# A 2x2x2 mean pool: all loads first on one DMA queue in 32 KB rows, all stores behind them

## The chip, the cores and the metric

The kernel runs on one core of a Trainium2 chip. Times are device microseconds (us) of one execution; lower is better. The kernel before takes 97.47 us, the median of three runs (97.29 to 97.55). A profile is one execution recorded by the hardware profiler; its span runs from the first to the last instruction of the program, and it is shorter than the measured time, because some time lies outside of it.

## What is computed

The input holds 8 x 32 volumes of 32 x 32 x 32 float32 numbers (33.55 MB). Each output number is the mean of a 2 x 2 x 2 block (4.19 MB in all).

```python
batch, channels, d, h, w = (8, 32, 32, 32, 32)
...
window = x[:, :, d_s:d_s + 2, h_s:h_s + 2, w_s:w_s + 2]
result[:, :, i, j, k] = np.mean(window, axis=(-3, -2, -1))
```

## The kernel before

The 256 volumes are taken in two halves of 128, one volume to a partition of the on-chip memory. A volume is a contiguous run of 128 KB in device memory. A half is cut along its depth into chunks of four planes (16 KB per partition, 2 MB over all partitions); the last chunk of the second half is cut again into two of two planes (8 KB per partition, 1 MB). There are 15 large and 2 small chunks.

`process_chunk` handles one chunk. Line 44 loads it, on the queue of SyncE (SP). VectorE (DVE) then makes three passes: line 50 adds planes in pairs (4096 numbers per partition become 2048), line 55 adds neighbours in a row (1024 are left), and line 59 adds rows in pairs, multiplies by 0.125 and writes 512 numbers into `obuf`, the output of the half; its unused sum goes to `dummy`, with a short instruction that reads the sum out. No other engine computes.

Outputs leave on the queue of ScalarE (ACT). When 14 of the 16 output planes of a half are done, line 91 stores them in one transfer (14 KB per partition, 1.84 MB). For the first half line 94 stores the other two planes in one transfer of 256 KB; for the second half lines 96 and 94 store one plane each (128 KB).

Three things set the order. SP issues loads in program order, and load n waits until the buffer that it reuses has been read by line 50: the pool `pin` has six buffers of 16 KB per partition, so up to six loads (12 MB) are queued. The stores stand on another queue, and run beside whatever loads are under way when they are issued. Each transfer also uses one of eight completion semaphores in turn (`DMAHW0` to `DMAHW7` below), and waits until its earlier user is done. Both queues feed the same 16 DMA engines.

Of the kernel before, what the change touches and what calls it, by code (L numbers as in the profile page):

```python
# [1 line left out]

# [4 lines left out]


@with_exitstack
def kernel(  # L10
    ctx: ExitStack,
    tc: tile.TileContext,
    x: bass.AP,
    kernel_size: int,
    out: bass.AP,
):
    nc = tc.nc
    assert kernel_size == 2, "only kernel_size == 2 supported"

    B, C, D, H, W = x.shape  # L20
    Do, Ho, Wo = D // 2, H // 2, W // 2
    N = B * C
    P = nc.NUM_PARTITIONS
    assert N % P == 0
    T = N // P

    xv = x.rearrange("b c d h w -> (b c) d h w")
    ov = out.rearrange("b c d h w -> (b c) d h w")

    HW = H * W  # L30

    add = mybir.AluOpType.add

    pool_in = ctx.enter_context(tc.tile_pool(name="pin", bufs=6))
    pool_mid = ctx.enter_context(tc.tile_pool(name="pmid", bufs=3))
    pool_out = ctx.enter_context(tc.tile_pool(name="pout", bufs=2))

    MAXDD = 4

    def process_chunk(xt, obuf, d0, DD, do0):  # L40
        OD = DD // 2
        tin_full = pool_in.tile([P, MAXDD * HW], mybir.dt.float32, tag="tin")
        tin = tin_full[:, : DD * HW]
        nc.sync.dma_start(out=tin, in_=xt[:, d0:d0 + DD, :, :])  # L44

        tin_v = tin.rearrange("p (od dd h w) -> p od dd h w", od=OD, dd=2, h=H, w=W)

        t1 = pool_mid.tile([P, (MAXDD // 2) * HW], mybir.dt.float32, tag="t1")
        t1 = t1[:, : OD * HW].rearrange("p (od h w) -> p od h w", od=OD, h=H, w=W)
        nc.vector.tensor_add(out=t1, in0=tin_v[:, :, 0], in1=tin_v[:, :, 1])  # L50

        t1_v = t1.rearrange("p od h (k ww) -> p od h k ww", ww=2)
        t2 = pool_mid.tile([P, (MAXDD // 2) * H * Wo], mybir.dt.float32, tag="t2")
        t2 = t2[:, : OD * H * Wo].rearrange("p (od h k) -> p od h k", od=OD, h=H, k=Wo)
        nc.vector.tensor_add(out=t2, in0=t1_v[:, :, :, :, 0], in1=t1_v[:, :, :, :, 1])  # L55

        t2_v = t2.rearrange("p od (j hh) k -> p od j hh k", hh=2)
        dummy = pool_mid.tile([P, 1], mybir.dt.float32, tag="dummy")
        nc.vector.tensor_tensor_reduce(  # L59
            out=obuf[:, do0:do0 + OD, :, :],  # L60
            in0=t2_v[:, :, :, 0, :],
            in1=t2_v[:, :, :, 1, :],
            scale=0.125,
            scalar=0.0,
            op0=add,
            op1=add,
            accum_out=dummy,
        )

    for t in range(T):  # L70
        xt = xv[t * P:(t + 1) * P]
        ot = ov[t * P:(t + 1) * P]

        obuf = pool_out.tile([P, Do, Ho, Wo], mybir.dt.float32, tag="obuf")

        if t == T - 1:
            chunks = [4] * (D // 4 - 1) + [2, 2]
            bulk_at = len(chunks) - 3
        else:
            chunks = [4] * (D // 4)  # L80
            bulk_at = len(chunks) - 2
        n = len(chunks)

        d0 = 0
        for ci, DD in enumerate(chunks):
            do0 = d0 // 2
            process_chunk(xt, obuf, d0, DD, do0)

            hi = do0 + DD // 2
            if ci == bulk_at:  # L90
                nc.scalar.dma_start(out=ot[:, 0:hi, :, :], in_=obuf[:, 0:hi, :, :])
            elif ci > bulk_at:
                if ci == n - 1:
                    nc.scalar.dma_start(out=ot[:, do0:, :, :], in_=obuf[:, do0:, :, :])
                else:
                    nc.scalar.dma_start(out=ot[:, do0:hi, :, :], in_=obuf[:, do0:hi, :, :])
            d0 += DD


# [1 line left out]
_INS = ['x', 'kernel_size']  # L101
_OUTS = [((8, 32, 16, 16, 16), 'float32')]
#: Inputs that are plain numbers.
_NUMBERS = {'kernel_size': 2}


# [26 lines left out]
```

## Time and profile before

| what | value |
|---|---|
| median of three runs | 97.47 us (97.29 to 97.55) |
| span of the profiled execution | 95.5 us |
| VectorE busy | 67.6 us (71% of the span), 68 instructions |
| data read and written | 33.55 MB and 4.19 MB, 395 GB/s over the span |
| queue of the loads (q1) | 2448 packets, 83.9% of 16 engines' span |
| queue of the stores (q10) | 720 packets, 10.6% of 16 engines' span |

The profile states no time of its own for the profiled execution beside the span. The span is 1.9 us below the median of the runs without a profiler, and this 1.9 us is taken as what lies around it. The three lines of digits in the page cut the span into 40 slices of 2.4 us: a digit is the busy share of a slice in tenths, and the row GB/s is what the DMA engines moved. A transfer's time "to landing" runs from its issue to the completion that the waiting engine sees. There is only one core, and its granted TensorE clock is 1.000 throughout; TensorE is not used.

### The profile page before, as it was taken

Reading aid. Unit: us, or ns where it says so; the run is one execution under the profiler, and the core shown is the slowest. Engines: PE = TensorE matmul, PEld = TensorE weight load, DVE = VectorE, ACT = ScalarE, POOL = GpSimd, SP = SyncE. Lnnn points to the kernel's source line nnn. Section 1 sums busy time; section 2 is a strip of 40 time slices with the busy share of each in tenths; the row PEclk is TensorE's granted clock in tenths of the full one; section 3 lists DMA queues with packets and bytes.
Section 4 is the critical chain, followed back from the end, with each engine's and each line's share of the span. In section 5 each row is a group of like instructions: output and inputs, shape, how many; then the busy total and the mean of one; then the engine's idle time right before and its main releaser. Section 6 shows DMA issues by size and latency. Waiting matters only on the chain.

```text
span 95.5 us, 151 instructions
## 1 busy us (share of the span) xinstructions
DVE 67.6 (71%) x68; POOL 0.2 (0%) x4
## 2 busy tenths in 40 slices
DVE  0006979797979797979439409879795979799920
POOL 0000000000000000000000000000000000000000
DMA  4899999999999999999999999999999999991993
GB/s 103 343 432 439 439 439 439 439 432 439 439 405 412 418 425 432 439 439 329 362 412 439 428 418 440 424 439 432 432 429 425 439 425 429 398 422 55 384 384 110
DMA packets 3169, 37.76 MB, mean 395 GB/s; under 512 B 352, under 2 KB 608, under 8 KB 736
## 3 DMA queue, kind: packets, MB, share of 16 engines
q1 hardware_dynamic: 2448, 33.56, 83.9%
q10 hardware_dynamic: 720, 4.19, 10.6%
q14 instruction: 1, 0.01, 0.0%
HBM read 33.55 MB, written 4.19 MB: 395 GB/s over the span
## 4 chain that ended last, share of the span: by engine, by line
DMA 79%; DVE 16%; issue 0%; SPq 0%; DVEq 0%
DMA tin_full<-in_x_dram 64%; DMA out_dram<-obuf 15%; DVE t L50 10%; DVE t L55 4%; DVE obuf L59 2%; DVE dummy L59 0%; SPq L44 0%; DVEq L128 0%
## 5 line engine op out<-in xcount | busy, mean ns | idle before, releaser
L50 DVE TENSOR_TENSOR t<-tin_full 128x2048 f32<-128x2048 f32 (+1 forms) x17 | 36.8, 2165 | 22.8 <-DMA tin_full<-in_x_dram 22.8
L55 DVE TENSOR_TENSOR t<-t 128x1024 f32<-128x1024 f32 (+1 forms) x17 | 19.7, 1162 | 0.5
L59 DVE CUSTOM_DVE_ANT_1 obuf<-t 128x512 f32<-128x512 f32 (+1 forms) x17 | 11.2, 660 | 0.5
L59 DVE DVE_READ_ACCUMULATOR2_ANT dummy<- 128x1 f32 x17 | 1.4, 82 | 0.0
L114 POOL MEMSET const-bfloat16-1.0<- 128x1 bf16 x1 | 0.1, 101 | 0.0
L114 POOL MEMSET const-uint8-127<- 128x1 uint8 x1 | 0.1, 101 | 0.0
L114 POOL MEMSET const-float32-0.0<- 128x1 f32 x1 | 0.1, 98 | 0.2 <-issue 0.2
L114 POOL MEMSET const-float32-1.0<- 128x1 f32 x1 | 0.1, 98 | 0.0
## 6 DMA issues: line engine op xcount, KB each, us to landing
tin_full<-in_x_dram SPq DMA_DIRECT2D x15, 2048.0 KB, 27.0
out_dram<-obuf ACTq DMA_DIRECT2D x2, 1792.0 KB, 10.1
tin_full<-in_x_dram SPq DMA_DIRECT2D x2, 1024.0 KB, 24.1
out_dram<-obuf ACTq DMA_DIRECT2D x1, 256.0 KB, 15.0
out_dram<-obuf ACTq DMA_DIRECT2D x2, 128.0 KB, 4.1
```

What stands on the lines that cost most here:

```text
L50: nc.vector.tensor_add(out=t1, in0=tin_v[:, :, 0], in1=tin_v[:, :, 1])
L55: nc.vector.tensor_add(out=t2, in0=t1_v[:, :, :, :, 0], in1=t1_v[:, :, :, :, 1])
L59: nc.vector.tensor_tensor_reduce(out=obuf[:, do0:do0 + OD, :, :], in0=t2_v[:, :, :, 0, :], in1=t2_v[:, :, :, 1, :], scale=0.125, scalar=0. ...
L114: nc = _bacc.Bacc("TRN2", target_bir_lowering=False, num_devices=1)
```

## The change

Loads now go to buffers of 32 KB per partition, eight planes (4 MB) each; the pool has five of them, 20 MB. A table `plan` lists eight such buffers: the first is filled by two transfers of 16 KB per partition, the next six by one transfer of 32 KB each, and the last by transfers of 16, 8 and 8 KB. DVE works on the same pieces as before, four planes at a time and two planes at the end (`pool_unit`), so that two units are cut out of one 32 KB transfer. The intermediates `t1` and `t2` have one buffer in place of three. The outputs of both halves stay in two buffers of 16 KB per partition, and all stores stand behind the last load in the program, on the same queue as the loads: the whole first half (2.10 MB), then 14 planes of the second half (1.84 MB), then its two last planes (131 KB each).

```diff
-    pool_in = ctx.enter_context(tc.tile_pool(name="pin", bufs=6))
-    pool_mid = ctx.enter_context(tc.tile_pool(name="pmid", bufs=3))
-    pool_out = ctx.enter_context(tc.tile_pool(name="pout", bufs=2))
...
+    pool_in = ctx.enter_context(tc.tile_pool(name="pin", bufs=5))
+    pool_mid = ctx.enter_context(tc.tile_pool(name="pmid", bufs=1))
+    pool_out = ctx.enter_context(tc.tile_pool(name="pout", bufs=1))
+    obuf = [pool_out.tile([P, 16 * KF], F32, name=f"obuf{t}") for t in range(2)]
+    plan = [
+        (0, 0, (16, 16)),
+        (0, 32, (32,)),
...
+        (1, 64, (32,)),
+        (1, 96, (16, 8, 8)),
+    ]
+    def load(t, k0, parts):
+        tin = pool_in.tile([P, 32 * KF], F32, tag="tin", name="tin")
+        o = 0
+        for kb in parts:
+            nc.sync.dma_start(
+                out=tin[:, o * KF:(o + kb) * KF],
+                in_=xv[t * P:(t + 1) * P, (k0 + o) * KF:(k0 + o + kb) * KF],
+            )
+            o += kb
+        return tin
...
+    for i, (t, k0, parts) in enumerate(plan):
+        tin = load(t, k0, parts)
+        o = 0
+        for kb in parts:
+            for u in range(0, kb, 16):
+                pool_unit(tin, t, k0, o + u, min(16, kb))
+            o += kb
...
-            if ci == bulk_at:
-                nc.scalar.dma_start(out=ot[:, 0:hi, :, :], in_=obuf[:, 0:hi, :, :])
...
+    for t, k0, kb in [(0, 0, 16), (1, 0, 14), (1, 14, 1), (1, 15, 1)]:
+        nc.sync.dma_start(
+            out=ov[t * P:(t + 1) * P, k0 * KF:(k0 + kb) * KF],
+            in_=obuf[t][:, k0 * KF:(k0 + kb) * KF],
+        )
```

`KF` is 256 numbers, 1 KB. `pool_unit` makes the three passes of `process_chunk` at lines 69, 74 and 78.

The first place is the tail of SP's program, from the load that reuses the third buffer to the end; the load lines are L44 before and L56 now, the stores are L95, and the semaphores and the DVE that a transfer waits for stand in brackets.

```order
-L44 DMA tin_full<-in_x_dram 128x4096 [waits DMAHW1_49,DMAHW0_49,DVE_49]
-L44 DMA tin_full<-in_x_dram 128x2048 [waits DMAHW3_49,DVE_49]
-L44 DMA tin_full<-in_x_dram 128x2048 [waits DMAHW4_49,DMAHW2_49,DVE_49]
-L128 UNCONDITIONAL_BRANCH
...
+L56 DMA tin<-in_x_dram 128x4096 [waits DMAHW3_49,DVE_49]
+L56 DMA tin<-in_x_dram 128x2048 x2
+L95 DMA out_dram<-obuf_64 128x4096 [waits DVE_49]
+L95 DMA out_dram<-obuf_65 128x3584 [waits DMAHW4_49,DVE_49]
+L95 DMA out_dram<-obuf_65 128x256 [waits DMAHW5_49,DVE_49]
+L95 DMA out_dram<-obuf_65 128x256 [waits DMAHW6_49,DVE_49]
+L129 UNCONDITIONAL_BRANCH
```

SP ended with its loads; now four stores stand behind them, each waiting for the DVE.

The second place is ACT's program, which held the five stores.

```order
-L91 DMA out_dram<-obuf 128x3584 [waits DMAHW0_49,DVE_49]
-L94 DMA out_dram<-obuf 128x512 [waits DMAHW2_49,DVE_49]
-L91 DMA out_dram<-obuf 128x3584 [waits DMAHW3_49,DVE_49]
-L96 DMA out_dram<-obuf 128x256 [waits DMAHW4_49,DVE_49]
-L94 DMA out_dram<-obuf 128x256 [waits DMAHW5_49,DVE_49]
```

None of them is left on that queue. The third place is DVE's end, where the last 16 KB piece of `tin` and the first 8 KB piece are worked on (t_169 and t_175 are intermediates).

```order
+L69 TENSOR_TENSOR t_169<-tin 128x2048 [waits DMAHW0_49]
+L74 TENSOR_TENSOR t_171<-t_169 128x1024 [waits DVE_49]
+L78 ISA obuf_65,dummy<-t_171 128x512 [waits DVE_49]
+L78 ISA dummy 128x1
+L69 TENSOR_TENSOR t_175<-tin 128x1024 [waits DMAHW1_49]
+L74 TENSOR_TENSOR t_177<-t_175 128x512 [waits DVE_49]
+L78 ISA obuf_65,dummy<-t_177 128x256 [waits DVE_49]
```

The same instructions stood there before, save that the pair addition of the 8 KB piece came one place earlier, ahead of the row addition of the 16 KB piece; now a unit ends before the next begins.

More of the change, by code (lines that the diff above doesn't have):

```diff
@@ L6 @@
 from concourse._compat import with_exitstack
+F32 = mybir.dt.float32
+KF = 256
 @with_exitstack
@@ L20 @@
     B, C, D, H, W = x.shape
-    Do, Ho, Wo = D // 2, H // 2, W // 2
-    N = B * C
     P = nc.NUM_PARTITIONS
[L24 to L30, printed above, removed]
-    add = mybir.AluOpType.add
-    pool_in = ctx.enter_context(tc.tile_pool(name="pin", bufs=6))
-    pool_mid = ctx.enter_context(tc.tile_pool(name="pmid", bufs=3))
-    pool_out = ctx.enter_context(tc.tile_pool(name="pout", bufs=2))
@@ L38 @@
[L38 to L67, printed above, removed]
-        )
@@ L70 @@
[L70 to L89, printed above, removed]
-            if ci == bulk_at:
[L91 to L97, printed above, removed]
+    assert (B * C, D, H, W) == (2 * P, 32, 32, 32)
@@ new lines @@
+    add = mybir.AluOpType.add
+    xv = x.rearrange("b c d h w -> (b c) (d h w)")
+    ov = out.rearrange("b c d h w -> (b c) (d h w)")
+    pool_in = ctx.enter_context(tc.tile_pool(name="pin", bufs=5))
[5 more added lines that the diff above has]
+        (0, 32, (32,)),
+        (0, 64, (32,)),
+        (0, 96, (32,)),
+        (1, 0, (32,)),
+        (1, 32, (32,)),
+        (1, 64, (32,)),
+        (1, 96, (16, 8, 8)),
+    ]
@@ new lines, in load, with pool_unit @@
+    def load(t, k0, parts):
[8 more added lines that the diff above has]
+        return tin
+    def pool_unit(tin, t, k0, o, kb):
+        od = kb // 8
+        a = tin[:, o * KF:(o + kb) * KF].rearrange("p (o dd e) -> p o dd e", o=od, dd=2)
+        t1 = pool_mid.tile([P, 8 * KF], F32, tag="t1", name="t1")
+        b = t1[:, :od * 1024]
+        nc.vector.tensor_add(
+            out=b.rearrange("p (o e) -> p o e", o=od), in0=a[:, :, 0], in1=a[:, :, 1])
+        bv = b.rearrange("p (e ww) -> p e ww", ww=2)
+        t2 = pool_mid.tile([P, 4 * KF], F32, tag="t2", name="t2")
+        c = t2[:, :od * 512]
+        nc.vector.tensor_add(out=c, in0=bv[:, :, 0], in1=bv[:, :, 1])
+        cv = c.rearrange("p (j hh k) -> p j hh k", hh=2, k=16)
+        dummy = pool_mid.tile([P, 1], F32, tag="dummy", name="dummy")
+        o0 = (k0 + o) * KF // 8
+        nc.vector.tensor_tensor_reduce(
+            out=obuf[t][:, o0:o0 + od * 256].rearrange("p (j k) -> p j k", k=16),
+            in0=cv[:, :, 0], in1=cv[:, :, 1],
+            scale=0.125, scalar=0.0, op0=add, op1=add, accum_out=dummy,
+        )
@@ L101 @@
+    tins = []
+    for i, (t, k0, parts) in enumerate(plan):
[10 more added lines that the diff above has]
+        )
 _INS = ['x', 'kernel_size']
```

## The prediction

> **What bounds the kernel now.** I read the page first: busy shares, slices, queues.
>
> ```profile
> span 95.5 us, 151 instructions
> DVE 67.6 (71%) x68; POOL 0.2 (0%) x4
> DMA  4899999999999999999999999999999999991993
> GB/s 103 343 432 439 439 439 439 439 432 439 439 405 412 418 425 432 439 439 329 362 412 439 428 418 440 424 439 432 432 429 425 439 425 429 398 422 55 384 384 110
> q1 hardware_dynamic: 2448, 33.56, 83.9%
> q10 hardware_dynamic: 720, 4.19, 10.6%
> ```
>
> The DMA engines are busy in nearly every slice, at a rate that rarely leaves 420 to 440 GB/s. DVE is idle for 29% of the span. So the bytes set the time, and what can be won is time in which the engines move less than they can: the ramp at the start, the dip in slices 18 to 20 (329, 362, 412), the hole in slice 36 (55) and the end. To size these I cut the span into stretches (columns: us, DVE busy and count, POOL, clock, DMA share, GB/s).
>
> ```profile
> 0.00:1.70 1.70, 0.00 (x0) 0.20 (x4) 1.00 0.00 0
> 4.00:42.10 38.10, 29.51 (x28) 0.00 (x0) 1.00 1.01 430
> 42.14:67.58 25.44, 16.86 (x16) 0.00 (x0) 1.00 1.00 412
> 67.58:82.74 15.16, 12.65 (x12) 0.00 (x0) 1.00 1.00 425
> 86.50:88.90 2.40, 2.37 (x5) 0.00 (x0) 1.00 0.02 7
> 88.90:94.20 5.30, 2.48 (x6) 0.00 (x0) 1.00 0.97 396
> 94.20:95.50 1.30, 0.00 (x0) 0.00 (x0) 1.00 0.00 0
> ```
>
> The last loads are through at 86.5, the last stores run from 88.9, and between them 2.40 us pass at 7 GB/s. The timeline tells why (start, duration, engine, line).
>
> ```profile
> 0.73 64.65 SPq L44 DMA_DIRECT2D tin_full<-in_x_dram  x17
> 7.89 2.29 DVE L50 TENSOR_TENSOR t<-tin_full 128x2048 f32<-128x2048 f32 x1 [7.89 <-DMA tin_full<-in_x_dram]
> 12.76 2.29 DVE L50 TENSOR_TENSOR t<-tin_full 128x2048 f32<-128x2048 f32 x1 [0.58 <-DMA tin_full<-in_x_dram]
> 37.24 2.29 DVE L50 TENSOR_TENSOR t<-tin_full 128x2048 f32<-128x2048 f32 x1 [0.61 <-DMA tin_full<-in_x_dram]
> 39.56 1.23 DVE L55 TENSOR_TENSOR t<-t 128x1024 f32<-128x1024 f32 x1
> 40.82 0.69 DVE L59 CUSTOM_DVE_ANT_1 obuf<-t 128x512 f32<-128x512 f32 x1
> 41.44 0.08 DVE L59 DVE_READ_ACCUMULATOR2_ANT dummy<- 128x1 f32 x1
> 41.55 0.38 ACTq L91 DMA_DIRECT2D out_dram<-obuf  x1
> 42.14 2.29 DVE L50 TENSOR_TENSOR t<-tin_full 128x2048 f32<-128x2048 f32 x1 [0.62 <-DMA tin_full<-in_x_dram]
> ...
> 67.58 2.29 DVE L50 TENSOR_TENSOR t<-tin_full 128x2048 f32<-128x2048 f32 x1 [0.57 <-DMA tin_full<-in_x_dram]
> 82.74 2.29 DVE L50 TENSOR_TENSOR t<-tin_full 128x2048 f32<-128x2048 f32 x1 [0.62 <-DMA tin_full<-in_x_dram]
> 88.07 0.34 ACTq L91 DMA_DIRECT2D out_dram<-obuf  x1
> 89.03 1.22 DVE L50 TENSOR_TENSOR t<-tin_full 128x1024 f32<-128x1024 f32 x1
> 91.36 0.08 DVE L59 DVE_READ_ACCUMULATOR2_ANT dummy<- 128x1 f32 x1
> 91.47 0.34 ACTq L94 DMA_DIRECT2D out_dram<-obuf  x1
> ```
>
> The second half's bulk store (L91 at 88.07) must wait for DVE, which got its chunk at 82.74 and is behind the loads at the end. The first half's store went out long before, at 41.55, into a stream of loads that already filled the engines: it gained nothing there, and nothing was left to fill the hole.
>
> **The rhythm.** From 12.76 to 42.14 DVE starts on six loads, always upon a landing: 29.38 / 6 = 4.897 us per 2 MB load (2.097 MB, so 428 GB/s). This is the price of a full stream. The lead ahead of it is 7.87 - 4.90 = 2.97 us. In 42.14 to 67.58 four loads land and the first half's 2.10 MB of stores leave, worth five such units, 24.49 us; it took 25.44, so 0.95 us is lost. In 67.58 to 82.74 three loads land, worth 14.69; 15.16 passed, 0.47 lost with no store about.
>
> **Stores: from issue to landing.**
>
> ```profile
> L91 ACTq DMA_DIRECT2D out_dram<-obuf x2: 339/359/379, 41.6 to 88.1; - x2
> DMA to landing us min/median/max: 5.9/10.1/14.4
> L94 ACTq DMA_DIRECT2D out_dram<-obuf x2: 338/338/338, 46.5 to 91.5; - x2
> DMA to landing us min/median/max: 3.1/9.1/15.0
> ```
>
> The bulk store of the end lands 5.9 us after issue; 1.835 MB at the stream's 428 GB/s is 4.29, so 1.6 lies around it. The very last lands at 91.47 + 3.1 = 94.57, and the span ends 0.93 later.
>
> **The change, part by part.** The bytes are the same. I follow the stream, and call T the landing of the last load.
>
> Loads: 16 units of 4.897 with nothing between them put T at 2.97 + 78.35 = 81.3. The supply holds: the five buffers are 20 MB, more than the 12 MB now queued, and DVE frees a buffer of 4 MB in 8.4 us (a unit is 41.44 - 37.24 = 4.20 us, and the next may start beside the read of the sum) while 4 MB take 9.79. The third buffer's units end near 2.97 + 29.4 + 8.4 = 41, so that the last loads are issued some 40 us ahead of their landing. The cover is DVE's 1.4 us per buffer; without it each buffer would add the difference.
>
> The 0.47 us lost without stores may come again, since nothing in it is touched: bounds 0 and 0.47, I take 0.25, halfway.
>
> Rows of 32 KB: six loads, 25.2 MB, become half as many packets. No row shows such a packet. The last 2.10 MB of stores, with 24 packets per engine (14 KB and 1 KB rows), took 5.30 against 4.90 at the full stream, a difference of 0.40 with its ramp, so at most 17 ns per packet; 48 packets fewer on each engine can gain at most 0.8. On the other side the mixed stretch, 412 GB/s against 428, is the slowest long one: 25.2 MB at 412 cost 61.1 in place of 58.8, +2.3. I take -0.2, because the DMA share of 1.01 in 4.00 to 42.10 shows packets abutting with no gap that longer ones would close.
>
> A rule that speaks for more: the Trainium skill, "DMA: Bandwidth & Descriptors", section "Anatomy of one DMA", puts about 2.0 us fixed cost on each DMA beside its bytes. Unhidden, 11 loads in place of 17 would give back 6 x 2.0 = 12 us by that page, an estimate that would put the time near 82; its own figure of 436 GB/s would make one 2 MB load 6.8 us alone, and the rhythm of 4.897 shows the fixed part hidden behind the queue, so by the trace it gives nothing.
>
> Switch from loads to stores in one queue: not seen in the trace. The nearest row is the stretch in which stores begin among loads, 0.95 lost in all; the other bound is 0, as loads follow loads. I take 0.2: there is one switch instead of 15 us of mixture.
>
> Stores: the first half's 2.10 MB were computed by about 2.97 + 4 x 9.79 + 8.4 = 51 and stand in the queue long before T, so they begin at once: 4.90. Meanwhile DVE works off what is left. The seventh buffer lands at T - 9.79; its two units end at T - 1.4, the 16 KB piece at T + 2.8, the two 8 KB pieces (91.36 - 89.03 = 2.33 each) at T + 5.1 and T + 7.5. The bulk store is issued at T + 2.9; the page's first load shows 1.0 from issue (0.73) to first bytes (1.70), so it is ready at T + 3.9, ahead of the end of the first store at about T + 4.5 (landing lags by 0.4 or so). The last is issued at T + 7.6, ready at T + 8.6, behind bulk bytes that run until T + 8.8. So the stores of the second half follow without a hole: 5.30 less 0.1 for the ramp that is gone, 5.2. Alone, the last store would land between T + 7.6 + 1.9 (1.6 around, 0.3 of bytes) = T + 9.5 and + 3.1 = T + 10.7, against T + 10.1 for the stream; nearly level, DVE is the next limit.
>
> Other edits, at nothing: single `t1` and `t2`, since DVE runs in order and the unit of 4.20 in the trace is already serial; SP's waits for DVE, behind which only stores stand.
>
> Sum: 81.3 + 0.25 - 0.2 + 0.2 + 4.9 + 5.2 + 0.93 = 92.6, against the span of 95.5: -2.9. Counted the other way, by what goes: the hole 2.40, the mixture 0.95, half of the 0.47 and 0.2 for the rows, less 0.2 for the switch, is -3.6. The two differ by how far a landing lags behind its last bytes at the end of the loads (I counted landing to landing), so I take the middle, -3.25: a span of 92.3. The median of the runs, 97.47, lies 1.9 above the span of before, and this stays: **94.2 us**.
>
> **Rivals.** *Late stores.* A store needs longer from issue to first bytes than 1.0. For: the first bulk store, issued at 41.55, took 14.4 to land, and 1.835 MB at half of 428 are 8.6, so up to 5.8 may be delay. With 4 us the bulk would start at T + 6.9, 2.4 late, and the end moves to 94.2 + 2.3 = 96.5. Against: 5.9 at the end, and the queue is the same one as the first store's.
>
> *The 0.95 belongs to writes, not to mixture.* Then it comes along: 94.2 + 0.95 - 0.2 = 95.0. For: 412 GB/s with stores about. Against: 5.30 for the last 2.10 MB loses only 0.40. The same page of the Trainium skill, section "Issuing engines are not separate DMA queues", says that transfers of all engines interleave on the same 16 DMA engines; by that rule the change of queue is worth nothing by itself and only the order counts, and the mixed stretch at 412 neither proves nor refutes it.
>
> *Long rows are slow (the other side).* If 32 KB rows run at the 396 GB/s of the last stretch in place of 428, 25.2 MB cost 63.6 instead of 58.8: 94.2 + 4.8 + 0.2 = 99.2. It decides from a loss of 3.3 us, 5% of the rate, on. For: no such row was ever seen. Against: 14 KB and 16 KB rows run alike, and 396 has short rows in it.
>
> *DVE sets the end*, no change. With one buffer for `t1` and `t2` a unit may take longer. At 4.8 in place of 4.2, DVE still keeps up with 9.79 per buffer but ends at T + 7.5 + 3 x 0.6 + 2 x 0.3 = T + 9.9; its last store, 3.1 later, lands at T + 13.0, 2.9 after the stream's end: 97.1. For: three buffers became one. Against: the serial unit of 4.20 above needed only one.
>
> **How the numbers follow.** Forecast 0.60, with 93.0 to 95.0 for it alone (0.8 less if the rows gain their bound and the switch is free, about as much more if the 0.47 and the 0.95 are both paid); writes 0.15 (95.0); late stores 0.11 (96.5); DVE 0.05 (97.1, which I count as no change, it may fall on either side); long rows 0.09 (99.2). About 0.3% is what a measurement of this kernel can tell from no change. Faster 0.60 + 0.15 + 0.11 = 0.86, same 0.05, slower 0.09. The range of 92.9 to 96.7 holds the first three, less some 0.05 that may lie below it.
>
> **What would show it.** Right: no slice under 350 GB/s between the first and the last ones, the first DVE waits spaced by 9.8 (or a little less), T near 81.3, no hole after it, the first store landing about 4.9 after T, the last about 10, DVE's units 4.2 apart within a buffer. Late stores: a hole behind the first store. Long rows: a spacing over 10.2. Wrong altogether: T above 85, or DVE running without waits from the middle on.

## The result, and the profile after

The changed kernel takes 94.98 us, the median of four runs (94.68 to 95.16), beside 97.38 for the kernel before: a ratio of 0.9756 with a 95% interval of 0.9731 to 0.978, so 2.4% faster. Forecast were 94.2 and a range of 92.9 to 96.7. The profiled execution is the fastest of the four (94.68, span 92.9); the spans of the others are 93.1 to 93.4.

The page of the changed kernel, lines as in the first view of the prediction:

```profile
span 92.9 us, 134 instructions
DVE 67.2 (72%) x68; POOL 0.2 (0%) x4
DMA  4899999999889999999999889999997999998990
GB/s 106 346 444 430 402 529 451 451 437 409 367 381 437 451 451 451 451 451 451 451 437 409 367 381 437 451 451 451 451 455 332 444 384 402 402 434 384 433 374 23
q1 hardware_dynamic: 2160, 37.75, 96.0%
```

The slice of 55 GB/s is gone. Loads and stores are one queue of 37.75 MB, and the engines work to the end of it. (A packet counts with all its bytes in the slice in which it starts; with packets of 32 KB that makes the row rise and fall in waves.) The timeline at the waits of DVE and the two groups of issues on SP:

```profile
0.73 39.38 SPq L56 DMA_DIRECT2D tin<-in_x_dram  x11
8.01 2.29 DVE L69 TENSOR_TENSOR t<-tin 128x2048 f32<-128x2048 f32 x1 [8.01 <-DMA tin<-in_x_dram]
12.91 2.29 DVE L69 TENSOR_TENSOR t<-tin 128x2048 f32<-128x2048 f32 x1 [0.61 <-DMA tin<-in_x_dram]
22.62 2.29 DVE L69 TENSOR_TENSOR t<-tin 128x2048 f32<-128x2048 f32 x1 [5.43 <-DMA tin<-in_x_dram]
26.83 2.29 DVE L69 TENSOR_TENSOR t<-tin 128x2048 f32<-128x2048 f32 x1
32.32 2.29 DVE L69 TENSOR_TENSOR t<-tin 128x2048 f32<-128x2048 f32 x1 [1.21 <-DMA tin<-in_x_dram]
...
50.54 39.01 SPq L95 DMA_DIRECT2D out_dram<-obuf  x4
...
61.46 2.29 DVE L69 TENSOR_TENSOR t<-tin 128x2048 f32<-128x2048 f32 x1 [1.23 <-DMA tin<-in_x_dram]
...
71.84 2.29 DVE L69 TENSOR_TENSOR t<-tin 128x2048 f32<-128x2048 f32 x1 [1.89 <-DMA tin<-in_x_dram]
```

From 22.62 to 61.46 four landings are 9.71 us apart, and the fifth takes 10.38. Within a buffer the units are 4.21 apart (22.62, 26.83). After 71.84 DVE waits for nothing more. The completion records of the trace give the rest: the last load lands at 82.19, the first half's store at 87.09, the bulk store of the second half at 91.35, the two small ones at 91.69 and 92.03. So the first store takes 4.90 after the last load, the full rate of the stream, and nothing stands between it and the next. The stretches show the two places where the rate is not full (columns as in the prediction's view):

```profile
22.60:61.44 38.84, 33.38 (x32) 0.00 (x0) 1.00 1.00 432
61.44:71.81 10.37, 8.34 (x8) 0.00 (x0) 1.00 0.99 426
78.00:80.00 2.00, 1.93 (x3) 0.00 (x0) 1.00 1.04 352
```

One is the late landing at 71.81. The other is a dip at 78 to 80, ahead of the first store: spread over their durations, the packets of the last loads move 379, 310 and 404 GB/s in the three microseconds from 78, and 431 after that. Packets of 8 KB that took 309 to 321 ns until then took up to 709 there.

### The profile page after: what moved, and what is told of

Read it like the earlier page. It is cut to its first block, busy times and chain, and to the rows that moved or that the text cites. A ratio compares the mean times of both kernels' runs of the same rounds, so it can differ in the third digit from the quotient of the medians.

```text
span 92.9 us, 134 instructions
## 1 busy us (share of the span) xinstructions
DVE 67.2 (72%) x68; POOL 0.2 (0%) x4
## 3 DMA queue, kind: packets, MB, share of 16 engines
q1 hardware_dynamic: 2160, 37.75, 96.0%
## 4 chain that ended last, share of the span: by engine, by line
DMA 68%; DVE 25%; SPq 1%; issue 1%; DVEq 0%
DMA tin<-in_x_dram 68%; DVE t L69 15%; DVE t L74 7%; DVE obuf L78 4%; SPq L56 1%; DVE dummy L78 0%; DVEq L129 0%
## 5 line engine op out<-in xcount | busy, mean ns | idle before, releaser
L69 DVE TENSOR_TENSOR t<-tin 128x2048 f32<-128x2048 f32 (+1 forms) x17 | 36.8, 2164 | 20.9 <-DMA tin<-in_x_dram 20.9
```

The costliest lines, as they stand in the source:

```text
L69: nc.vector.tensor_add(out=b.rearrange("p (o e) -> p o e", o=od), in0=a[:, :, 0], in1=a[:, :, 1])
```

## The experiments

Theory A says that order makes the gain: a store that is ready and stands behind the loads fills the time in which DVE works off what has landed. Its rivals give the gain to the longer rows and deeper buffers, or to having one queue. Two further questions came from the profile: the landing that is 0.66 late, and the dip. All ratios are to the kernel before, run on the same chip.

| kernel | time, us | ratio (95% interval) |
|---|---|---|
| before | 97.38 | |
| changed | 94.98 | 0.9756 (0.9731 to 0.978) |
| changed, stores on ACT | 99.30 | 1.0194 (1.0176 to 1.0212) |
| changed, 16 KB rows | 94.85 | 0.9738 (0.972 to 0.9757) |
| before, first half's store behind the loads | 94.83 | 0.9737 (0.9719 to 0.9756) |
| changed, units of 32 KB | 93.91 | 0.9642 (0.9623 to 0.9662) |
| changed, DVE instructions added | 95.05 | 0.9741 (0.9707 to 0.9776) |
| units of 32 KB, end 16 and 16 | 94.11 | 0.964 (0.9613 to 0.9666) |
| units of 32 KB, first store left out | 92.6, one run | |
| units of 32 KB, 16 KB rows | 94.50 | 0.9683 (0.9656 to 0.971) |
| units of 32 KB, last 8.4 MB of full buffers in 16 KB rows | 93.85 | 0.9634 (0.961 to 0.9658) |

### The same kernel with its stores on ACT

```diff
-        nc.sync.dma_start(
+        nc.scalar.dma_start(
             out=ov[t * P:(t + 1) * P, k0 * KF:(k0 + kb) * KF],
```

> The changed kernel with one edit: its four stores are issued on ACT's queue instead of SP's, each as soon as its data is computed. Theory A (the gain is that the first half's store fills the hole behind the loads): now it goes out at about 51 us among the loads, the last load lands 4.9 us later than the 82.2 of the changed kernel, at about 87, no store is left to cover DVE's lag, the bulk store waits until 2.9 us after that landing and a hole of 3 to 4 us opens; the time goes back to 97 to 98 us. Rival B (the gain is the 32 KB rows or the deeper buffering; the place of the stores does not matter, because the engines move the same bytes): the time stays at 95 us.

It is 1.9% slower than the kernel before. The 97 to 98 of theory A fits its span of 97.5; the 1.8 us around the span had been left out. The stretches of its tail:

```profile
51.70:86.00 34.30, 25.14 (x25) 0.00 (x0) 1.00 0.99 412
86.00:91.00 5.00, 4.93 (x5) 0.00 (x0) 1.00 0.06 23
91.00:96.00 5.00, 3.62 (x8) 0.00 (x0) 1.00 0.96 394
```

The first half's store, issued at 50.54, goes among the loads and lands at 69.36, and the rate there is again 412. So it is the place in the loads' own queue that keeps a ready store behind them. Then 5 us pass at 23 GB/s while DVE is busy throughout (4.93 of 5.00). The hole is longer than before's 2.40, because DVE's lag is: the last load lands at 87.23 and the bulk store goes out 2.9 later, at 90.1, where before it was 0.4 later (88.07 against 87.66). So rows and buffers of 32 KB do not make the gain; without the order they lose. The store behind the loads covers that lag as well as the old hole.

### The same kernel with rows of 16 KB

```diff
-    pool_in = ctx.enter_context(tc.tile_pool(name="pin", bufs=5))
+    pool_in = ctx.enter_context(tc.tile_pool(name="pin", bufs=10))
-        tin = pool_in.tile([P, 32 * KF], F32, tag="tin", name="tin")
+        tin = pool_in.tile([P, 16 * KF], F32, tag="tin", name="tin")
...
+    plan = [(t, k, (16,)) for t in range(2) for k in range(0, 128, 16)][:-1]
+    plan += [(1, 112, (8, 8))]
```

> The changed kernel with loads in rows of 16 KB (ten buffers of 16 KB, the same 20 MB; the last buffer in two loads of 8 KB rows); the stores stay behind the loads on SP. Theory A: the spacing of landings goes from 9.71 us per 4 MB back to 9.79, which is 0.5 us over six loads; the time is 95.2 to 95.6. Rival B (long rows and few transfers make the gain): 97 us or more. Rival C (rows make nothing): 95.0, with the spacing as before at 4.90 per 2 MB but no later end.

The spacing is back at 4.89 per 2 MB, as theory A and rival C expected, but the end is not later, as C alone said: 94.85, below A's 95.2 to 95.6, the interval overlapping that of the changed kernel. Its profile says what pays for it:

```profile
78.00:80.00 2.00, 1.97 (x2) 0.00 (x0) 1.00 1.04 434
```

The last load lands at 82.20 (82.19 in the changed kernel), since here the dip is missing: 434 in place of 352. DVE's lag is missing too: the bulk store is issued at 81.59, 0.6 before the last load lands, so the lag comes with landings of 4 MB.

### The kernel before with one store moved

```diff
-            if ci == bulk_at:
+            if t == 0:
+                pass
+            elif ci == bulk_at:
...
+        if t == 0:
+            held.append((ot, obuf))
+    for ot, obuf in held:
+        nc.sync.dma_start(out=ot[:, :, :, :], in_=obuf[:, :, :, :])
```

> The kernel before with one edit: the first half's output leaves in one store of 2.10 MB behind the last load on SP's queue; loads, rows of 16 KB, six buffers and the second half's stores on ACT's queue are as before. Theory A (order alone makes the gain): the hole of 2.40 us behind the loads and the 0.95 of mixing go, the last load lands at about 82.5; the time is 95.0 to 95.8. Rival B (one queue for everything is needed, because the second half's stores on their own queue start late beside the first store, 4 us from issue): 96 to 97. Rival C (rows or buffers make the gain): 97.4.

This one edit gives 94.83, the whole gain, just below the 95.0 to 95.8 of theory A; the interval overlaps that of the changed kernel. The loads, the rows, the six buffers of 16 KB, the two queues at the end are those of before. Rivals B and C fall. Its stores in the timeline:

```profile
59.61 0.42 SPq L104 DMA_DIRECT2D out_dram<-obuf  x1
...
82.63 0.38 ACTq L94 DMA_DIRECT2D out_dram<-obuf  x1
83.70 0.34 ACTq L99 DMA_DIRECT2D out_dram<-obuf  x1
86.04 0.34 ACTq L97 DMA_DIRECT2D out_dram<-obuf  x1
```

The first half's store is issued at 59.61 and runs behind the last load, which lands at 82.22. The bulk store of the second half comes from ACT at 82.63 and lands 8.7 later, at 91.33; the one of the changed kernel landed at 91.35. A queue of its own for it made nothing better and nothing worse.

### Fewer DVE instructions

In the changed kernel one packet of 8 KB on the instruction queue falls just ahead of the late landing. It starts at 69.16 and takes 0.32 us. The load packet that starts as it ends, at 69.47, takes 1875 ns, where packets of 32 KB usually take 1213: 0.66 more, just what the landing is late. The trace has sixteen completion records for each transfer; of those of the late load fifteen are together and the last comes 0.66 after them, and so it stays for the next two loads. The queues in 68 to 71 us:

```profile
q1 hardware_dynamic: 59, 1.15, 90.5%
q14 instruction: 1, 0.01, 0.7%
```

```diff
-    pool_in = ctx.enter_context(tc.tile_pool(name="pin", bufs=5))
+    pool_in = ctx.enter_context(tc.tile_pool(name="pin", bufs=4))
-        t1 = pool_mid.tile([P, 8 * KF], F32, tag="t1", name="t1")
+        t1 = pool_mid.tile([P, 16 * KF], F32, tag="t1", name="t1")
-        t2 = pool_mid.tile([P, 4 * KF], F32, tag="t2", name="t2")
+        t2 = pool_mid.tile([P, 8 * KF], F32, tag="t2", name="t2")
-            for u in range(0, kb, 16):
-                pool_unit(tin, t, k0, o + u, min(16, kb))
+            for u in range(0, kb, 32):
+                pool_unit(tin, t, k0, o + u, min(32, kb))
```

> The changed kernel with DVE working on a whole 32 KB buffer at a time where one transfer fills it (11 units in place of 17, so 44 DVE instructions in place of 68; four buffers of 32 KB in place of five, for lack of room). In the changed kernel one 8 KB packet of the instruction queue q14 runs at 69.2 us, and the landing that follows is 0.66 late (10.37 in place of 9.71). Theory A: the packet fetches DVE's next instructions over one of the 16 DMA engines and that engine never catches up; with 44 instructions it is not needed before the end, every spacing is 9.71 and the time is 0.4 to 0.7 lower, 94.3 to 94.6. Rival B (the late landing has to do with the data's place in memory, or with the clock time): the spacing of 10.37 stays where it is and the time is 95.0. Four buffers may cost: a hole in the loads would show it.

93.91: lower by 1.1, more than the 0.4 to 0.7 expected. The list of its queues over the whole span, and its last waits:

```profile
q1 hardware_dynamic: 2160, 37.75, 96.8%
```

```profile
51.83 4.42 DVE L69 TENSOR_TENSOR t<-tin 128x4096 f32<-128x4096 f32 x1 [1.70 <-DMA tin<-in_x_dram]
61.55 4.42 DVE L69 TENSOR_TENSOR t<-tin 128x4096 f32<-128x4096 f32 x1 [1.69 <-DMA tin<-in_x_dram]
71.26 4.42 DVE L69 TENSOR_TENSOR t<-tin 128x4096 f32<-128x4096 f32 x1 [1.70 <-DMA tin<-in_x_dram]
```

There is no instruction packet within the span, and the spacing stays at 9.71 to the end. Four buffers are enough. The profiled executions differ by 0.8 in their spans (92.1 against 92.9): the landing is worth 0.6 and a smaller dip the rest.

### More DVE instructions

```diff
         o0 = (k0 + o) * KF // 8
+        tiny = pool_mid.tile([P, 1], F32, tag="tiny", name="tiny")
+        for _ in range(4):
+            nc.vector.memset(tiny, 0.0)
```

> The changed kernel with 68 one-column memsets more on DVE (into an unused tile; the scheduler puts 50 of them ahead of the first addition, where DVE waits 8 us for data, and most of the rest after the first unit). They cost DVE little, but its instruction count from the start reaches any given number some 60 instructions earlier. Theory A (the 8 KB packet of q14 brings DVE's next instructions, and the landing after it is late by 0.5 to 0.8 us on account of it): the packet and the late landing move together from 69 us to before the third landing, ahead of 25 us; every later spacing is 9.71, the end stays where it is, 94.7 to 95.2, since one fetch remains. Rival B (the late landing belongs to a place in memory or a clock time): it stays at 69 to 72 us, wherever the packet goes.

The packet moved to 10.36 us, and the late landing with it: the second load lands 5.62 after the first, where 4.90 is usual, and all later spacings are 9.71. Its queues in 9 to 12 us, and then its waits:

```profile
q1 hardware_dynamic: 78, 1.28, 100.4%
q14 instruction: 1, 0.01, 0.6%
```

```profile
23.26 2.29 DVE L69 TENSOR_TENSOR t<-tin 128x2048 f32<-128x2048 f32 x1 [5.19 <-DMA tin<-in_x_dram]
...
62.12 2.29 DVE L69 TENSOR_TENSOR t<-tin 128x2048 f32<-128x2048 f32 x1 [1.23 <-DMA tin<-in_x_dram]
...
71.82 2.29 DVE L69 TENSOR_TENSOR t<-tin 128x2048 f32<-128x2048 f32 x1 [1.22 <-DMA tin<-in_x_dram]
```

At 23.26 it is 0.64 behind the changed kernel's 22.62, at 71.82 level with its 71.84. Neither a place in memory nor a clock time moves with DVE's instruction count, so rival B falls. In all six kernels that have such a packet within the span, the load packet that starts as it ends takes 0.54 to 0.66 us longer than others of its size (1166 ns in place of 611 here). That the packet holds DVE's instructions is inferred from the name of its queue and from this run; fetching them once costs the stream 0.5 to 0.8 us. The kernel before pays it too. The 0.47 that the prediction found without a store about is this, as is the 0.82 of the kernel with 16 KB rows (5.72 in place of 4.90).

### What makes the dip

Four kernels with units of 32 KB, and so without the fetch, are set beside the one above, which has the dip. The first loads the last buffer in two rows of 16 KB; its two last planes leave in one store.

```diff
-        (1, 96, (16, 8, 8)),
+        (1, 96, (16, 16)),
...
-    for t, k0, kb in [(0, 0, 16), (1, 0, 14), (1, 14, 1), (1, 15, 1)]:
+    for t, k0, kb in [(0, 0, 16), (1, 0, 14), (1, 14, 2)]:
```

> The kernel with 32 KB units, and its last buffer loaded in two rows of 16 KB instead of 16, 8 and 8; the last two output planes leave in one store of 256 KB. In the changed kernel and in that with 32 KB units the rate falls to 306 to 310 GB/s for a microsecond, 2 us before the stores begin, while rows of 8 KB arrive. Theory A (the short rows behind 32 KB rows, with a store behind them, cause the dip; it costs 0.46 us): the dip is gone or below 0.2, the last load lands at 80.9 to 81.1 against 81.33, and the time is 93.3 to 93.7 against 93.9. Rival B (the switch from loads to a store in one queue costs the 0.46 whatever the rows): the dip stays and the time is 93.8 to 94.0.

The dip stays; its stretch:

```profile
78.00:80.00 2.00, 2.00 (x3) 0.00 (x0) 1.00 0.98 319
```

The last load lands at 81.33, as with the end of 16, 8 and 8, and the time is the same within the intervals. So short rows at the end are not the cause. The second never stores the first half's output, which is left out of its result.

```diff
-    for t, k0, kb in [(0, 0, 16), (1, 0, 14), (1, 14, 1), (1, 15, 1)]:
+    for t, k0, kb in [(1, 0, 14), (1, 14, 1), (1, 15, 1)]:
```

> The kernel with 32 KB units, but the first half's output is never stored (its 2.10 MB stay on the chip, so the stores are those of the second half alone). It tells where the dip ahead of the stores comes from. Theory A (the dip comes from the store that stands in the queue behind the last loads): no dip at 78 to 80 us, the last load lands at 80.8 to 81.0 against 81.33, then a hole of 3 us until the bulk store, and an end near 88.5 to 89.5 in the profile. Rival B (the dip comes from the rows of 8 KB themselves): the dip stays, the last load lands at 81.3.

```profile
78.00:80.00 2.00, 2.00 (x3) 0.00 (x0) 1.00 1.02 426
81.00:84.00 3.00, 2.93 (x5) 0.00 (x0) 1.00 0.00 0
```

No dip; the last load lands at 80.94, and then 3 us pass without a byte, the hole that the store would fill. (The end at 90.8 is later than the 88.5 to 89.5 expected: the bulk store lands at 89.19, the last small one at 89.89, and the span ends 0.94 after that.) Here the first store is issued at 83.35, when all loads have landed. So a store that waits in the queue behind the loads is a condition. The third fills each 32 KB buffer by two loads.

```diff
+        rows = (16, 16) if parts == (32,) else parts
-        for kb in parts:
+        for kb in rows:
```

> The kernel with 32 KB units, but each 32 KB buffer is filled by two loads with rows of 16 KB; the end is 16, 8, 8 as before. In the kernel with 16 KB rows there was no dip ahead of the stores. Theory A (32 KB rows gain 0.5 us on the way and lose 0.46 in the dip): spacing 4.89 per 2 MB, no dip, the last load at 81.2 to 81.4, and the time equal to that of 32 KB rows, 93.8 to 94.0. Rival B (the dip has nothing to do with the length of the earlier rows): the dip stays and the time is 94.3 to 94.5.

```profile
78.00:80.00 2.00, 1.97 (x4) 0.00 (x0) 1.00 1.01 414
```

Next to no dip, the last load at 81.42 and a span of 92.2, as theory A expected. The first store lands at 86.27 with both row lengths, so the 32 KB rows have given back what they gained. The time is 94.50 all the same, which rival B had given for another reason: 2.2 us lie around the span of its profiled execution (94.37) where 1.8 do with the 32 KB rows (93.84 and 92.1). That is not in the trace and stays open; the kernel with 16 KB rows and small units has 1.8. A last kernel has 16 KB rows in the sixth and seventh buffers alone.

```diff
+        rows = (16, 16) if (t, k0) in ((1, 32), (1, 64)) else parts
-        for kb in parts:
+        for kb in rows:
```

> The kernel with 32 KB units, but the sixth and seventh buffers are each filled by two loads with rows of 16 KB (8.4 MB of short rows between the 32 KB rows and the end; the end is 16, 8, 8). The dip ahead of the stores came with 32 KB rows earlier in the queue and a store behind it, and was nearly gone with 16 KB rows throughout. Theory A (what matters is the length of the rows in the last few loads before the store): the dip is gone, the last load lands at 81.0 to 81.1 against 81.33 and the profile ends at 91.7 to 91.9 against 92.1; the time is 0.965 to 0.960 of the kernel before. Rival B (32 KB rows leave the 16 DMA engines out of step with one another, and nothing later brings them together): the dip stays, at 310 to 340 GB/s, and the last load lands at 81.3 to 81.5.

```profile
78.00:80.00 2.00, 1.97 (x4) 0.00 (x0) 1.00 1.00 365
```

The dip is there, and the last load lands at 81.65, even a little behind what B said. The time, 93.85, is level with that of 32 KB rows. The table is made from the completion records: how long the last 2.10 MB of loads took, from one landing to the other, in all eleven kernels.

| kernel | long rows earlier | store waiting behind in the queue | us for the last 2.10 MB |
|---|---|---|---|
| before | no | no | 4.94 |
| changed, stores on ACT | yes | no | 4.95 |
| units of 32 KB, first store left out | yes | no | 4.96 |
| changed, 16 KB rows | no | yes | 4.95 |
| before, store moved | no | yes | 4.94 |
| units of 32 KB, 16 KB rows | no | yes | 4.97 |
| changed | yes | yes | 5.49 |
| changed, DVE instructions added | yes | yes | 5.88 |
| units of 32 KB | yes | yes | 5.21 |
| units of 32 KB, end 16 and 16 | yes | yes | 5.43 |
| units of 32 KB, last full buffers in 16 KB rows | yes | yes | 5.36 |

The stretch is longer, by 0.3 to 0.9, only where both meet. What happens in the engines is open. That 32 KB rows leave the 16 engines out of step until the end would fit the last kernel, but the completion records speak against it. For the load just ahead of this stretch, the sixteen records lie within 0.27 to 0.46 us in the three kernels that have a dip and no fetch, and within 0.41 in the one with 16 KB rows and units of 32 KB, which has next to none; in the two others with 16 KB rows and a store waiting, where the fetch came first, they lie 1.14 and 1.21 apart, and there is no dip. No run has long rows and a store that waits on another queue, so whether it must be the same queue is open too.

## Why the prediction was right, point by point

**The bound and the hole.** Right: the bytes set the time, and what could be won was the hole behind the loads and the loss beside the store. The moved store alone shows it, with everything else as before. Of the signs named, two did not come: a slice of 332 GB/s, the dip, lies below the 350, and one spacing is 10.38, the fetch.

**The loads.** T, the landing of the last load, was put at 81.3 + 0.25 - 0.2 + 0.2, and came at 82.19, 0.6 later. The rhythm and the supply were right; the first landing came 0.1 later than before (7.98 against 7.87). The term for the 32 KB rows was too small: 9.71 in place of 9.79 per buffer is 0.5 over six, where 0.2 was taken, inside the bound of 0.8. The term for the 0.47 lost without stores was mis-sized and not understood: 0.25 was taken, and it came back whole, 0.66 here, because it is the fetch of DVE's instructions over an engine of the full stream. The Trainium skill, "DMA: Bandwidth & Descriptors", section "Why a DMA increments its semaphore by 16 and not by 1", says that a transfer runs on up to 16 engines that finish independently, and that only the full count means all data landed. The trace agrees: of the sixteen completion records of the late landing fifteen are in when the last comes, 0.66 later. The switch from loads to stores was taken at 0.2 and cost 0.54 (5.49 against 4.95); with 16 KB rows it costs nothing. Too little was taken for two costs (by 0.41 and 0.34) and for one gain (by 0.28); that they partly cancel is luck.

**The stores.** Right: 4.90 after T for the first, and no hole behind it; 9.84 for the last against 10.1. The bulk store found its place in the queue in time, so "late stores" fell for the loads' own queue. On ACT beside the loads the delay exists: from the issue of the first store to its first bytes 4.0 us pass in the kernel before, and 4.9 with all stores on ACT. "The 0.95 belongs to writes" fell too: the first two stores, 3.93 MB, landed within 9.16 us of T, at 429 GB/s. "DVE sets the end" did not occur, with units of 4.21; "long rows are slow" fell by the spacing of 9.71.

**The fixed cost by the Trainium skill.** The page, "DMA: Bandwidth & Descriptors", section "Anatomy of one DMA", gives the 2.0 us for transfers issued from GpSimd, and here SP issues them. The 12 us that an estimate from it gave for 11 loads in place of 17 did not appear: 17 loads and 11 loads take 94.85 and 94.98.

**The sum.** The count along the stream gave a span of 92.6, the count by what goes 91.9, and I took the middle, 92.3. The first was nearer: 92.9 in the profile. The 0.6 from 92.3, with the profiled execution being 0.3 below its own median and 0.1 less around the span, is the 0.8 between 94.2 and 94.98. The mis-sized terms stand in both counts. The second also took the hole as 2.40, from last bytes to first bytes. From landing to landing it was worth 2.0: before, the last store lands 6.94 after the last load, with bytes worth 4.90; now 9.84 after it, with bytes worth 9.79.

**What was not seen.** The rest of the change, without the order, is a loss that the order hides. Landings of 4 MB make DVE's last bulk store 2.5 us later after the last load than before (2.9 against 0.4). I worked that lag out for the store's place in the queue, but not what it would cost with no store ahead: 1.9% slower than before.

## What to carry to other kernels

In a stream bound by bytes, an output that is ready early is worth most where nothing else can move: hold it on the chip, and put it behind the last load, so that it covers the work on the last data. Check what else uses the engines of a full stream: fetched instructions cost as well, and fewer, larger instructions took off about 1 us here, 0.6 of it the fetch. Where two parts of a change are made together, ask what each does alone.

## What had not been expected of the hardware

One 8 KB packet on the instruction queue, seen when DVE has begun 46 to 53 instructions, delays a full stream by 0.5 to 0.8 us through a single load packet on one engine (1875 ns in place of 1213); the five kernels with 44 DVE instructions or fewer never had it within the span. Rows of 32 KB move 0.8% faster than rows of 16 KB (9.71 against 9.79 us per 4 MB), and give it back ahead of a store that waits behind them in the same queue; why is open. The best kernels here, with units of 32 KB, take 93.85 to 93.91, 3.6 to 3.7% under the kernel before and 1.2% under the changed one.
